# Loading rows of k four to a partition, with the column order restored in three ways

## The chip, the cores and the metric

The kernel runs on one core of one Trainium2 chip. The metric is the device time of one execution in microseconds (us), the lower the better.

## The reference

Rotary embedding on q and k, then scores of every query row against every key row, for each head. All in fp32.

```python
batch, seq, heads, dim = 16, 512, 16, 64
q_rot = concat([q1 * cos - q2 * sin, q1 * sin + q2 * cos], axis=-1)   # halves of 32
k_rot = concat([k1 * cos - k2 * sin, k1 * sin + k2 * cos], axis=-1)
scores = np.einsum('bshd,bthd->bsht', q_rot, k_rot)                   # [16, 512, 16, 512]
```

The scores are 268 MB, q and k together 67 MB: the outputs are four times the inputs.

## The kernel before

The unit of work is a *block*: 128 rows of q of one batch against all 512 rows of k, all 16 heads, 4 MB of scores. A batch has four blocks (C = 4), the run 64. q's rows lie four to a partition (row 4p + c), k's rows the other way (row 128c + p), so that k's transposed columns come out in their natural order. The price is that k can be read from HBM only in runs of 4 KB.

```python
q_v = q.rearrange("b (p c) h d -> b p c h d", c=C)
k_v = k.rearrange("b (c p) h d -> b p c h d", c=C)
o_v = out.rearrange("b (p c) h t -> b c p h t", c=C)
# ... (cut)
def load_pair(which, pair):                       # 1 MB: half a batch
    b, x = divmod(pair, C // 2)
    # ...
    src = (k_v if which == "k" else q_v)[b, :, 2 * x : 2 * x + 2]
    nc.sync.dma_start(t.rearrange("p c (h d) -> p c h d", h=H), src)
```

VectorE (DVE) rotates each piece in three passes into a separate tile, TensorE (PE) transposes it, ScalarE (ACT) or DVE copies the transposes to `kT` and `qT`. Then the scores, a head pair at a time, on two 64-row halves of PE side by side (eight of these instructions took 1.92 us in the trace):

```python
def scores(i, p, st):
    # ... (cut)
    for r in range(2):
        nc.tensor.matmul(out=ps[:, r, :], lhsT=lhs[64 * r : 64 * r + 64, :],
                         rhs=rhs[64 * r : 64 * r + 64, :], start=True, stop=True)
    nc.scalar.copy(out=st[:, 2 * p : 2 * p + 2, :], in_=ps)
    # ...
    elif b > 0 and p == HP - 1:
        nc.sync.dma_start(o_v[b, i % C], st)      # one 4 MB store per block
```

There are three staging tiles `st`. One 1 MB load is issued after each block.

## Time and profile before

| | before |
|---|---|
| time, median of 3 | 808.65 us (808.45 to 809.09) |
| share of the DMA queue's packets in 16 engines' time | 98.2% |
| PE, ACT, DVE busy | 85%, 69%, 65% |
| one block in the steady stretch | 12.46 us |
| one block when nothing but PE limits it | 10.02 us |

In the profile's lines, "L172" is the source line of an instruction, `out<-in` names what is written and read, "x8" is a count. The chain of waits goes back from the last instruction to what released each step. The prediction shows its lines and reads them. Three more, of the page (after the "|": us busy, mean ns of one, us idle before and what ended it):

```profile
DMA 61%; PE 27%; ACT 6%; DVE 2%; issue 1%; ACTq 0%
...
L179 ACT COPY st<-ps 128x1024 f32<-128x1024 f32 x512 | 494.8, 1019 | 213.5 <-DMA out_dram<-st 145.1
L172 PE MATMUL ps<-kT_t,qT_t 64*128 64x512 f32 x2048 | 546.5, 647 | 82.6 <-ACT st L179 82.6
```

### The profile page before, as it was taken

What the parts mean: (1) busy time and instruction counts of PE and PEld (TensorE: products, weight loads), DVE (VectorE), ACT (ScalarE), POOL (GpSimd) and SP (SyncE); (2) the same over time, 40 slices, a digit from 0 to 9 for tenths busy, and PEclk for the clock granted to TensorE, in tenths of its full rate; (3) what the DMA queues carried; (4) which work ended last, traced back from release to release, by engine and by line L of the source; (5) the groups of instructions that cost most, each with busy time, mean ns of one, the idle gap of its engine ahead of it and who ended that gap; (6) DMA issues with size and microseconds to landing.
All of it is one profiled execution on the core that took longest, in us unless ns stands there. A gap on an engine that the chain in (4) does not pass through costs nothing.

```text
span 809.9 us, 7719 instructions
## 1 busy us (share of the span) xinstructions
PE 689.5 (85%) x3072; PEld 295.6 (36%) x3072; DVE 522.6 (65%) x508; ACT 561.8 (69%) x649; POOL 0.7 (0%) x6
## 2 busy tenths in 40 slices
PE   4989998898888888888879799797988989889870
PEld 3444443343333333333334333343333333333320
DVE  7899786655767656756568575576755856565400
ACT  4888886676767776767767668676767666777670
POOL 0000000000000000000000000000000000000000
PEclk9999999989999999999999999998989899999895
DMA  9999999999999999999999999999999999999995
GB/s 346 424 424 441 410 420 435 431 419 439 433 420 437 430 423 436 431 424 438 430 422 436 431 424 438 425 429 437 387 431 398 426 410 430 388 367 392 412 415 222
DMA packets 26916, 336.31 MB, mean 415 GB/s; under 512 B 3328, under 2 KB 4608, under 8 KB 13312
## 3 DMA queue, kind: packets, MB, share of 16 engines
q1 hardware_dynamic: 25536, 335.55, 98.2%
q8 instruction: 24, 0.39, 0.2%
q10 hardware_dynamic: 1344, 0.26, 0.2%
q14 instruction: 12, 0.10, 0.0%
HBM read 67.37 MB, written 268.44 MB: 415 GB/s over the span
## 4 chain that ended last, share of the span: by engine, by line
DMA 61%; PE 27%; ACT 6%; DVE 2%; issue 1%; ACTq 0%
DMA out_dram<-st 61%; PE ps L172 20%; PE bank L149 7%; ACT st L179 6%; DVE part L131 1%; DMA cos_k<-in_cos_dram 1%; DVE kT_t L229 0%; DVE q_rot L134 0%; DVE k_rot L134 0%; DVE k_rot L128 0%; DVE q_rot L128 0%; ACTq L300 0%; ACTq L179 0%
## 5 line engine op out<-in xcount | busy, mean ns | idle before, releaser
L179 ACT COPY st<-ps 128x1024 f32<-128x1024 f32 x512 | 494.8, 1019 | 213.5 <-DMA out_dram<-st 145.1
L172 PE MATMUL ps<-kT_t,qT_t 64*128 64x512 f32 x2048 | 546.5, 647 | 82.6 <-ACT st L179 82.6
L172 PEld LDWEIGHTS ps<-kT_t,qT_t 64*128 64x128 f32 x2048 | 180.7, 195 | 277.8 <-ACT st L179 145.5
L128 DVE TENSOR_TENSOR q_rot<-q_sb,cos_q 128x1024 f32<-128x1024 f32 x60 | 73.3, 1221 | 163.4 <-DMA q_sb<-in_q_dram 163.4
L267 DVE COPY qT_t<-bank 128x512 f32<-128x512 f32 x118 | 80.9, 686 | 78.9 <-PE bank L149 78.7
L149 PEld LDWEIGHTS bank<-ident,q_rot 128*128 128x128 f32 x512 | 60.3, 154 | 106.8 <-issue 85.6
L149 PE MATMUL bank<-ident,q_rot 128*128 128x128 f32 x512 | 92.8, 311 | 2.6 <-DVE q_rot L134 2.6
L149 PE MATMUL bank<-ident,k_rot 128*128 128x128 f32 x512 | 83.8, 288 | 11.1 <-DVE k_rot L134 10.8
L149 PEld LDWEIGHTS bank<-ident,k_rot 128*128 128x128 f32 x512 | 54.6, 142 | 104.9 <-issue 52.2
L134 DVE TENSOR_TENSOR k_rot<-k_rot,part 128x1024 f32<-128x1024 f32 x64 | 78.3, 1224 | 2.1
L134 DVE TENSOR_TENSOR q_rot<-q_rot,part 128x1024 f32<-128x1024 f32 x64 | 77.8, 1215 | 0.2
L128 DVE TENSOR_TENSOR k_rot<-k_sb,cos_k 128x1024 f32<-128x1024 f32 x60 | 73.1, 1218 | 0.0
L131 DVE TENSOR_TENSOR part<-k_sb,ss_k 128x1024 f32<-128x1024 f32 x60 | 73.0, 1217 | 0.0
L131 DVE TENSOR_TENSOR part<-q_sb,ss_q 128x1024 f32<-128x1024 f32 x60 | 72.9, 1215 | 0.0
L269 ACT COPY kT_t<-bank 128x512 f32<-128x512 f32 x112 | 66.8, 597 | 0.0
L128 DVE TENSOR_TENSOR k_rot<-early,cos_k 128x1024 f32<-128x1024 f32 x4 | 4.9, 1220 | 5.0 <-DMA cos_k<-in_cos_dram 5.0
L189 ACT COPY qT_t<-bank 128x512 f32<-128x512 f32 x10 | 5.6, 616 | 3.0 <-PE bank L149 3.0
L189 ACT COPY kT_t<-bank 128x512 f32<-128x512 f32 x10 | 5.5, 604 | 2.0 <-PE bank L149 2.0
L229 DVE COPY kT_t<-bank 128x512 f32<-128x512 f32 x6 | 4.1, 686 | 2.6 <-PE bank L149 2.6
L128 DVE TENSOR_TENSOR q_rot<-early,cos_q 128x1024 f32<-128x1024 f32 x4 | 4.9, 1217 | 0.0
L131 DVE TENSOR_TENSOR part<-early,ss_q 128x1024 f32<-128x1024 f32 x4 | 4.9, 1216 | 0.0
L131 DVE TENSOR_TENSOR part<-early,ss_k 128x1024 f32<-128x1024 f32 x4 | 4.9, 1215 | 0.0
(11 smaller groups left out, 3.4 us busy)
## 6 DMA issues: line engine op xcount, KB each, us to landing
out_dram<-st SPq DMA_DIRECT2D x60, 4096.0 KB, 27.7
k_sb<-in_k_dram SPq DMA_DIRECT2D x30, 1024.0 KB, 30.2
q_sb<-in_q_dram SPq DMA_DIRECT2D x30, 1024.0 KB, 28.8
out_dram<-st SPq DMA_DIRECT2D x16, 1024.0 KB, 11.3
early<-in_k_dram SPq DMA_DIRECT2D x1, 1536.0 KB, 9.1
early<-in_q_dram SPq DMA_DIRECT2D x1, 1536.0 KB, 12.4
early<-in_k_dram SPq DMA_DIRECT2D x1, 512.0 KB, 4.0
early<-in_q_dram SPq DMA_DIRECT2D x1, 512.0 KB, 5.5
```

What stands on the lines that cost most here:

```text
L128: lambda: nc.vector.tensor_tensor(a.rearrange(v1, **k1), src.rearrange(sv, j=HD), cs, op=mult),
L131: lambda: nc.vector.tensor_tensor(bt.rearrange(v1, **k2), src.rearrange(sv, j=D), ss, op=mult),
L134: lambda: nc.vector.tensor_tensor(a4, a4, swapped, op=add),
L149: nc.tensor.transpose(bank[:, x, :], src, ident)
L172: nc.tensor.matmul(out=ps[:, r, :], lhsT=lhs[64 * r : 64 * r + 64, :], rhs=rhs[64 * r : 64 * r + 64, :], start=True, stop=True,)
L179: nc.scalar.copy(out=st[:, 2 * p : 2 * p + 2, :], in_=ps)
L189: nc.scalar.copy(out=dst, in_=bank)
L229: nc.vector.tensor_copy(out=dst, in_=bank)
L267: nc.vector.tensor_copy(out=dst, in_=bank)
L269: nc.scalar.copy(out=dst, in_=bank)
```

## The change

The intent: read k as q is read, four rows to a partition, so that whole batches come in single 2 MB loads with runs of 16 KB; rotate in place, which frees the tiles for the rotated copies. But then column 128c + p of the transposed k belongs to row 4p + c, and the scores' columns must be put right: by PE's read of k, by PE's write to PSUM, or by ACT's read of PSUM. The change uses each in a third of the batches.

```diff
-    k_v = k.rearrange("b (c p) h d -> b p c h d", c=C)
+        "k": k.rearrange("b (p c) h d -> b p c h d", c=C),
 ...
+        t = in_pool.tile([P, C, H * D], fp32, tag=which + "_in", name=which + "_sb")
+        batches[which, b] = t
+        nc.sync.dma_start(t.rearrange("p c (h d) -> p c h d", h=H), dram[which][b])
 ...
+        def products():
+            nc.vector.tensor_tensor(pv, xs, ss, op=mult)
+            nc.vector.tensor_tensor(xc, xc, cs, op=mult)          # in place
 ...
         for r in range(2):
+            po, rh = ps[:, r, :], rhs[64 * r : 64 * r + 64, :]
+            if b > 0 and b % 3 == 1:                              # PE reads with a hop
+                rh = rh.rearrange("e (c t) -> e t c", c=C)
+                po = po.rearrange("s (t c) -> s t c", c=C)
+            elif b > 0 and b % 3 == 2:                            # PE writes with a step
+                rh = rh.rearrange("e (c t) -> e c t", c=C)
+                po = po.rearrange("s (t c) -> s c t", c=C)
 ...
+        if b > 0 and b % 3 == 0:                                  # ACT reads with a hop
+            so = so.rearrange("s r (t c) -> s r t c", c=C)
+            si = si.rearrange("s r (c t) -> s r t c", c=C)
 ...
-            if i % 2 == 1:
-                load_pair("q", (i + 1) // 2 + 2)
-            else:
-                load_pair("k", (i + 4) // 2 + 3)
+            if i % C == C - 2:
+                load("q", i // C + 2)
+            elif i % C == C - 1:
+                load("k", i // C + 3)
```

The first batch, which is loaded by heads, restores its order in the copies of the transposes; it is left out here.

More of the change, by code (lines that the diff above doesn't have):

```diff
@@ L34 @@
     in_pool = ctx.enter_context(tc.tile_pool(name="in", bufs=2))
-    rot_pool = ctx.enter_context(tc.tile_pool(name="rot", bufs=2))
+    part_pool = ctx.enter_context(tc.tile_pool(name="part", bufs=1))
     kt_pool = ctx.enter_context(tc.tile_pool(name="kt", bufs=2))
@@ L40 @@
     ps_t_pool = ctx.enter_context(tc.psum_pool(name="ps_t", bufs=2))
-    q_v = q.rearrange("b (p c) h d -> b p c h d", c=C)
-    k_v = k.rearrange("b (c p) h d -> b p c h d", c=C)
+    dram = {
+        "q": q.rearrange("b (p c) h d -> b p c h d", c=C),
+        "k": k.rearrange("b (p c) h d -> b p c h d", c=C),
+    }
     o_v = out.rearrange("b (p c) h t -> b c p h t", c=C)
     ident = const_pool.tile([P, P], fp32, name="ident")
-    tabs = {}
-    def load_tables(which, pat):
-        for name, src in (("cos", cos), ("sin", sin)):
-            t = const_pool.tile([P, C, HD], fp32, name=f"{name}_{which}")
-            nc.scalar.dma_start(t, src.rearrange(pat, c=C))
-            tabs[name, which] = t
-    def build_table(which):
-        ss = const_pool.tile([P, C, 2, HD], fp32, name=f"ss_{which}")
-        nc.scalar.copy(out=ss[:, :, 0, :], in_=tabs["sin", which])
-        nc.scalar.mul(ss[:, :, 1, :], tabs["sin", which], -1.0)
-        tabs["ss", which] = ss.rearrange("p c x j -> p c (x j)")
-    in_tiles = {}
-    IN_BUFS = {"k": 3, "q": 2}
-    def in_tile(which, pair):
-        t = in_pool.tile(
-            [P, 2, H * D], fp32, tag=which + "_in", bufs=IN_BUFS[which], name=which + "_sb"
-        )
-        in_tiles[which, pair] = t
-        return t
+    cos_t = const_pool.tile([P, C, HD], fp32, name="cos_t")
+    sin_t = const_pool.tile([P, C, HD], fp32, name="sin_t")
+    ss_t = const_pool.tile([P, C, 2, HD], fp32, name="ss_t")
+    ss_v = ss_t.rearrange("p c x j -> p c (x j)")
     st_first = [stage_pool.tile([P, H, S], fp32, tag="stage", name="st") for _ in range(2)]
@@ L77 @@
     units = {}
+    used = [0]
     def load_units(which, head, heads):
         n = C * heads * D
-        t = early[:, load_units.used : load_units.used + n]
-        load_units.used += n
-        t = t.rearrange("p (c e) -> p c e", c=C)
-        src = (k_v if which == "k" else q_v)[0, :, :, head : head + heads, :]
+        t = early[:, used[0] : used[0] + n].rearrange("p (c e) -> p c e", c=C)
+        used[0] += n
+        src = dram[which][0, :, :, head : head + heads, :]
         nc.sync.dma_start(t.rearrange("p c (h d) -> p c h d", d=D), src)
@@ L87, in load_units, with load @@
             units[which, (head + h) // G] = t[:, :, D * h : D * (h + G)]
-    load_units.used = 0
-    def load_pair(which, pair):
-        b, x = divmod(pair, C // 2)
+    batches = {}
+    def load(which, b):
         if b >= B:
             return
-        t = in_tile(which, pair)
-        src = (k_v if which == "k" else q_v)[b, :, 2 * x : 2 * x + 2]
-        nc.sync.dma_start(t.rearrange("p c (h d) -> p c h d", h=H), src)
-    rots = {}
+        t = in_pool.tile([P, C, H * D], fp32, tag=which + "_in", name=which + "_sb")
+        batches[which, b] = t
+        nc.sync.dma_start(t.rearrange("p c (h d) -> p c h d", h=H), dram[which][b])
@@ L102, in rope @@
     def rope(which, n):
-        a = rot_pool.tile([P, H * D], fp32, tag="rot_" + which, name=which + "_rot")
-        bt = rot_pool.tile([P, H * D], fp32, tag="part", name="part")
-        cs, ss = tabs["cos", which], tabs["ss", which]
+        part = part_pool.tile([P, H * D], fp32, tag="part", name="part")
         if n < C:
-            src = units[which, n]
-            sv = "p c (g j) -> p c g j"
-            v1 = "p (c g j) -> p c g j"
-            k1 = {"c": C, "j": HD}
-            cs = cs.unsqueeze(2).to_broadcast((P, C, 2 * G, HD))
-            ss = ss.unsqueeze(2).to_broadcast((P, C, G, D))
-            k2 = {"c": C, "j": D}
-        else:
-            src = in_tiles[which, n // 2][:, n % 2]
-            sv = "p (g j) -> p g j"
-            v1 = "p (g j) -> p g j"
-            k1 = {"j": HD}
-            cs = cs[:, n % C].unsqueeze(1).to_broadcast((P, 2 * H, HD))
-            ss = ss[:, n % C].unsqueeze(1).to_broadcast((P, H, D))
-            k2 = {"j": D}
@@ L124, in rope @@
-        swapped = bass.AP(bt.tensor, bt.offset + HD, [bt.ap[0], (D, H), (-HD, 2), (1, HD)])
-        a4 = a.rearrange("p (h x j) -> p h x j", x=2, j=HD)
-        rots[which, n] = a
-        return [
-            lambda: nc.vector.tensor_tensor(
-                a.rearrange(v1, **k1), src.rearrange(sv, j=HD), cs, op=mult
-            ),
-            lambda: nc.vector.tensor_tensor(
-                bt.rearrange(v1, **k2), src.rearrange(sv, j=D), ss, op=mult
-            ),
-            lambda: nc.vector.tensor_tensor(a4, a4, swapped, op=add),
-        ]
+            x = units[which, n]
@@ new lines, in rope @@
+            sv, k1, k2 = "p c (g j) -> p c g j", {"j": HD}, {"j": D}
+            cs = cos_t.unsqueeze(2).to_broadcast((P, C, 2 * G, HD))
+            ss = ss_v.unsqueeze(2).to_broadcast((P, C, G, D))
+            pv = part.rearrange("p (c g j) -> p c g j", c=C, j=D)
+            x5 = x.rearrange("p c (h x j) -> p c h x j", x=2, j=HD)
+            p5 = part.rearrange("p (c h x j) -> p c h x j", c=C, x=2, j=HD)
+            adds = [(x5[:, :, :, y], p5[:, :, :, 1 - y]) for y in range(2)]
+        else:
+            x = batches[which, n // C][:, n % C]
+            sv, k1, k2 = "p (g j) -> p g j", {"j": HD}, {"j": D}
+            cs = cos_t[:, n % C].unsqueeze(1).to_broadcast((P, 2 * H, HD))
+            ss = ss_v[:, n % C].unsqueeze(1).to_broadcast((P, H, D))
+            pv = part.rearrange(sv, **k2)
+            x4 = x.rearrange("p (h x j) -> p h x j", x=2, j=HD)
+            swapped = bass.AP(part.tensor, part.offset + HD, [part.ap[0], (D, H), (-HD, 2), (1, HD)])
+            adds = [(x4, swapped)]
@@ L137, with sums, transposed @@
+        xs, xc = x.rearrange(sv, **k2), x.rearrange(sv, **k1)
+        def products():
+            nc.vector.tensor_tensor(pv, xs, ss, op=mult)
+            nc.vector.tensor_tensor(xc, xc, cs, op=mult)
+        def sums():
+            for y, z in adds:
+                nc.vector.tensor_tensor(y, y, z, op=add)
+        return [products, sums]
     kT = {}
     qT = {}
-    def transposed(which, n, g):
-        rot = rots[which, n]
+    def transposed(which, n, g, copy):
         bank = ps_t_pool.tile([P, 4, P], fp32, tag="ps_t", name="bank")
@@ L145, in transposed @@
             if n < C:
-                src = rot.rearrange("p (c e) -> p c e", c=C)[:, x, P * g : P * (g + 1)]
+                src = units[which, n][:, x, P * g : P * (g + 1)]
             else:
-                src = rot[:, P * (4 * g + x) : P * (4 * g + x + 1)]
+                src = batches[which, n // C][:, n % C, P * (4 * g + x) : P * (4 * g + x + 1)]
             nc.tensor.transpose(bank[:, x, :], src, ident)
+        src = bank
         if which == "q":
@@ L157, in transposed @@
                 kT[b] = kt_pool.tile([P, HP, S], fp32, tag="kT", name="kT_t")
-            t = kT[b].rearrange("p h (c t) -> p h c t", c=C)
-            dst = t[:, 2 * n + g] if n < C else t[:, 4 * g : 4 * g + 4, n % C]
-        return bank, dst
+            if n < C:
+                dst = kT[b][:, 2 * n + g].rearrange("p (t c) -> p t c", c=C)
+                src = bank.rearrange("p c t -> p t c")
+            else:
+                dst = kT[b][:, 4 * g : 4 * g + 4, P * (n % C) : P * (n % C + 1)]
+        copy(out=dst, in_=src)
     def scores(i, p, st):
@@ L171, in scores @@
         for r in range(2):
-            nc.tensor.matmul(
-                out=ps[:, r, :],
-                lhsT=lhs[64 * r : 64 * r + 64, :],
-                rhs=rhs[64 * r : 64 * r + 64, :],
-                start=True,
-                stop=True,
-            )
-        nc.scalar.copy(out=st[:, 2 * p : 2 * p + 2, :], in_=ps)
+            po, rh = ps[:, r, :], rhs[64 * r : 64 * r + 64, :]
[5 more added lines that the diff above has]
+                po = po.rearrange("s (t c) -> s c t", c=C)
+            nc.tensor.matmul(
+                out=po, lhsT=lhs[64 * r : 64 * r + 64, :], rhs=rh, start=True, stop=True
+            )
+        so, si = st[:, 2 * p : 2 * p + 2, :], ps
+        if b > 0 and b % 3 == 0:
+            so = so.rearrange("s r (t c) -> s r t c", c=C)
+            si = si.rearrange("s r (c t) -> s r t c", c=C)
+        nc.scalar.copy(out=so, in_=si)
         if b == 0 and p % 2 == 1:
@@ L187, in tr_act @@
         for g in range(2):
-            bank, dst = transposed(which, n, g)
-            nc.scalar.copy(out=dst, in_=bank)
+            transposed(which, n, g, nc.scalar.copy)
     def run(ops):
@@ L195 @@
     with tc.manual_schedule():
-        load_tables("k", "(c p) j -> p c j")
-        load_tables("q", "(p c) j -> p c j")
+        for t, src in ((cos_t, cos), (sin_t, sin)):
+            nc.scalar.dma_start(t, src.rearrange("(p c) j -> p c j", c=C))
         for head, heads in ((0, G), (G, H - G)):
@@ L200 @@
             load_units("q", head, heads)
-        load_pair("k", 2)
-        load_pair("q", 2)
-        load_pair("k", 3)
+        load("k", 1)
+        load("q", 1)
         make_identity(nc, ident)
-        build_table("k")
-        build_table("q")
-        run(rope("k", 0))
-        tr_act("k", 0)
-        run(rope("q", 0))
-        tr_act("q", 0)
+        nc.scalar.copy(out=ss_t[:, :, 0, :], in_=sin_t)
+        nc.scalar.mul(ss_t[:, :, 1, :], sin_t, -1.0)
+        for which in ("k", "q"):
+            run(rope(which, 0))
+            tr_act(which, 0)
         for i in range(C):
             st = st_first[i] if i < 2 else stage_pool.tile([P, H, S], fp32, tag="stage", name="st")
-            late = []
-            if i > 0:
-                late = [("k", C + i - 1, 0), ("k", C + i - 1, 1)]
             if i < C - 1:
@@ L225 @@
                 scores(i, p, st)
-                if p in (0, 1) and late:
-                    bank, dst = transposed(*late.pop(0))
-                    dve.pop(0)()
-                    nc.vector.tensor_copy(out=dst, in_=bank)
-                if i == 0 and p == 1:
-                    load_pair("k", 4)
-                if i == 0 and p == 3:
-                    load_pair("q", 3)
+                if p in (0, 1) and i > 0:
+                    run(dve[:1])
+                    dve = dve[1:]
+                    transposed("k", C + i - 1, p, nc.vector.tensor_copy)
+                if p == 3 and i < 2:
+                    load("kq"[i], 2)
                 if p in (2, 6):
-                    m = len(dve) - (6 if p == 2 else 3) + (-3 if i == C - 1 else 0)
+                    m = len(dve) - (4 if p == 2 else 2) - (2 if i == C - 1 else 0)
                     run(dve[:m])
@@ L239 @@
             run(dve)
-            if i == 1:
-                load_pair("k", 5)
-            elif i == 3:
-                load_pair("q", 4)
-                load_pair("k", 6)
+        load("k", 3)
         for i in range(C, NST):
@@ L262 @@
                     continue
-                bank, dst = transposed(*tr[p])
                 if tr[p][0] == "q":
@@ L266 @@
                     dve = dve[1:]
-                    nc.vector.tensor_copy(out=dst, in_=bank)
+                    transposed(*tr[p], nc.vector.tensor_copy)
                 else:
-                    nc.scalar.copy(out=dst, in_=bank)
+                    transposed(*tr[p], nc.scalar.copy)
             run(dve)
-            if i % 2 == 1:
-                load_pair("q", (i + 1) // 2 + 2)
-            else:
-                load_pair("k", (i + 4) // 2 + 3)
+            if i % C == C - 2:
+                load("q", i // C + 2)
+            elif i % C == C - 1:
+                load("k", i // C + 3)
 _INS = ['q', 'k', 'cos', 'sin']
```

## The prediction

> **What bounds the kernel now.** I read the page's head and DMA parts first, then the chain of waits, the timeline of a steady stretch and the waits. First: is any resource full?
>
> ```profile
> PE 689.5 (85%) x3072; PEld 295.6 (36%) x3072; DVE 522.6 (65%) x508; ACT 561.8 (69%) x649; POOL 0.7 (0%) x6
> ...
> DMA packets 26916, 336.31 MB, mean 415 GB/s; under 512 B 3328, under 2 KB 4608, under 8 KB 13312
> ...
> q1 hardware_dynamic: 25536, 335.55, 98.2%
> ```
>
> No compute engine is full; the DMA queue's packets fill 98.2% of the 16 engines' time. Inputs and outputs together are 335.5 MB, so the change cannot lower the bytes. Second: does the end hang on those transfers? The chain of waits in order of time (start, length, what) repeats one figure from about 120 us on:
>
> ```profile
> 158.18 28.73 DMA out_dram<-st
> ...
> 187.01 1.02 ACT st L179
> ...
> 196.08 28.20 DMA out_dram<-st
> ...
> 233.46 28.18 DMA out_dram<-st
> ```
>
> A 4 MB store takes about 28 us from issue to landing; its staging buffer is then refilled in 9.1 us (187.01 to 196.08) and stored again. There are three buffers, so one 4 MB block of scores passes each (233.46 - 196.08) / 3 = 12.46 us. With 1.05 MB of loads per block that is 5.24 MB / 12.46 us = 421 GB/s. Third: what can the compute do when no buffer is missing? The same chain earlier, before the staging buffers bind:
>
> ```profile
> 72.70 1.92 PE ps L172 x8
> ...
> 82.71 1.92 PE ps L172 x8
> ...
> 92.73 1.92 PE ps L172 x8
> ```
>
> The same place in the block recurs every 10.02 us, with PE busy throughout. So PE has 2.4 us to spare per block. Of the 10.02 us, 8 x 0.96 = 7.7 us are scores (1.92 us for 8 instructions, and four instructions are one head pair of scores) and 4 x 0.59 are transposes. ACT needs 8 copies of 1.02 us or slightly less in succession, plus two of 0.60 us: at most 9.4 us. Fourth, the waits between 160 and 484 us:
>
> ```profile
> DVE q_rot L128 <- DMA q_sb<-in_q_dram: 79.7, 13, 6.7
> ACT st L179 <- DMA out_dram<-st: 73.3, 26, 4.0
> PEld ps L172 <- ACT st L179: 68.9, 52, 3.6
> ```
>
> ACT waits 2.8 us per block for a store: that is the DMA bound seen from ACT. The longest wait, DVE for q, is the tempting one, 163 us over the run, but those rotations run a block ahead and PE loses almost nothing by it in the steady stretch.
>
> [...] the median 4 KB packet took 159 ns, 8 KB 309 ns, 32 KB 1213 ns. From 8 to 32 KB this is 904 / 24 = 37.7 ns per KB, which leaves about 8 ns fixed per packet. [...]
>
> **The change part by part.**
>
> Loads. Before, k came in 4 KB packets (30 loads of 1 MB, 256 packets each, 7,680 in all) and q in 8 KB (3,840). After, 30 loads of 2 MB carry 3,840 packets of 16 KB. A 16 KB packet should take 309 + 8 x 37.7 = 610 ns (an estimate from the two rows). Before: (7,680 x 159 + 3,840 x 309) / 16 = 76.3 + 74.2 = 150.5 us of all engines. After: 3,840 x 610 / 16 = 146.4 us. Saved: 4.1 us. Thirty fewer DMAs drop 480 completion packets of 9 ns: 0.3 us. As DMA is the bound, these 4.4 us come off the end.
>
> Prefetch. A q batch is now asked for at the end of the third block of a batch for use four blocks later, some 3 blocks or 37 us before DVE wants it, against a landing of about 30 us. So DVE's q wait should nearly vanish. It wasn't on the bound; I book 0 to 4 us for the irregular stretch from 560 to 690 us, where blocks took about 12.85 us (599.89 - 561.36 = 38.5 us per three).
>
> Rotation in place. Again three DVE passes of 1,024 elements (1.22 us each); for the first batch the sum becomes two halves of 512. Nothing on the bound: DVE stays at about 520 us. [...]
>
> Column order. k's row 4p+c now becomes column 128c+p of its transpose, and each block must put it right. In batches 1, 4, 7, 10, 13 PE reads k with a hop of 512 bytes at every element; in 2, 5, 8, 11, 14 PE writes PSUM with a step of 16 bytes; in 3, 6, 9, 12, 15 ACT reads PSUM with a hop of 512 bytes. Twenty blocks each. The sizes are the same and no instruction is added, so cost comes only from a slower element rate. Call the factor on the score matmuls f: a block takes 7.7 f + 2.36 us of PE, which reaches the DMA's 12.4 us at f = 1.30. For ACT, 8.2 f + 1.2 reaches it at f = 1.37.
>
> There is also a cushion. When a buffer comes free, two other stores and some loads still stand in the queue, 2 x 4.19 MB + 1.05 MB at 421 GB/s = 22 us, while refilling takes 9 us. So about 13 us of lateness are absorbed before the DMA idles, and each unhindered block wins back 2.4 us. At f = 1.7 in the PE-read batches alone, a block is 15.4 us, 12 us late per batch, absorbed and won back in the next eight blocks: cost near 0. At f = 2, 17.7 us: 21 us late, 8 over the cushion, times 5 batches: 40 us. At 1.7 in both PE ways, 24 us late with only four blocks (10 us) to recover: 14 x 5 = 70 us. At 1.7 in all three, ACT's block is 15.1 us, nothing is recovered, and (12 + 12 + 11) x 5 = 175 us come on.
>
> **The rivals.** (1) All three orders are free, or slow by less than 30%: 808.7 - 4.4 = 804 us, perhaps 800. [...] (2) One way is slow and the cushion hides it: 805 to 820; the page would show the slower instruction and an unchanged end. (3) The PE read at twice the time: PE becomes the bound in those batches, about 845. (4) Two or three ways slow: 870 to 980. (5) The loads, now in bursts of 2 MB, leave gaps in the queue: unlikely, as even two stores alone hold 20 us of work against 9 us of refilling.
>
> **Range and chances.** I give (1) about 0.40 and (2) 0.17, which make "within 2%" or, with luck in the irregular stretch, faster; (3) and (4) share 0.42. For more than 2% faster, 16 us would have to be found where I count 4 to 8: 0.04. The median of this lopsided mix lies a little above the free case, at 812 us; the range goes from a clean 798 to 915.
>
> **What would show it.** The page should list 16 KB loads of 2 MB, the DVE wait for q near zero, and blocks of about 12.4 us. The three kinds of score instructions settle the rest, by batch: matmuls of about 0.24 us effective in every batch and ACT copies of 1.02 us mean rival (1). Longer ones with gaps in the DMA row in the same batches mean (3) or (4). I'm wrong altogether if the blocks change length while the score instructions and the queue's packets do not, or if the packets of 16 KB take much other than 610 ns.

The sum is 808.7 - 4.4 = 804 us if all three orders are free, with 0 to 4 us less for the prefetch, and 0, 40, 70 or 175 us more if they are not. The factors 1.7 and 2 in the latter are assumed, and the chances are the author's estimate; nothing in the trace before showed how fast such an access is.

## The result and the profile after

The changed kernel took 855.22 us (median of 4, 851.76 to 855.62) against 808.59 us (808.45 to 809.09). The ratio is 1.0566, 95% interval 1.0538 to 1.0594. Here and below a ratio is the mean time of one kernel's fast runs over the mean of the other's in the same rounds, so it is not quite the ratio of the quoted medians. The times of the kernel before varied between 804.7 and 813.3 us in the later rounds.

The page after, in the parts that answer to those shown of before:

```profile
PE 794.1 (93%) x3072; PEld 292.3 (34%) x3072; DVE 544.9 (64%) x516; ACT 567.5 (67%) x647; POOL 0.7 (0%) x6
...
GB/s 355 423 415 416 275 261 359 438 425 435 424 437 310 372 414 428 432 425 435 335 346 394 431 427 439 422 438 274 372 419 433 432 425 436 316 370 419 419 430 364
...
q1 hardware_dynamic: 17376, 335.55, 93.8%
...
PE 78%; DMA 14%; DVE 3%; ACT 2%; issue 0%; ACTq 0%; DVEq 0%
```

There are 8,160 fewer packets, as planned, for the same bytes. But PE went from 689.5 to 794.1 us busy with the same 3,072 matmuls, and the end now hangs on PE (78% of the chain, DMA 14%; before 27% and 61%). The GB/s row has five holes: slices of 261 to 372 where the others, the first and the last apart, have 394 and more. Five batches read k on PE with the hop, at even distances. The chain of waits shows the block in such a batch, and then in the next one (start, length, what):

```profile
238.29 3.67 PE ps L161 x8
...
255.31 3.67 PE ps L161 x8
...
297.60 1.92 PE ps L161 x8
...
307.62 1.92 PE ps L161 x8
```

The same place in the block recurs every 17.02 us in batch 4, and every 10.02 us in batch 5, which writes PSUM with the step. Eight score instructions took 3.67 us in the one and 1.92 us in the other. For the whole cycle of batches 4, 5, 6 (from the last store of batch 3 to that of batch 6) the view by windows gives the columns: us, busy time of PE, PE's weight loads, DVE, ACT and POOL, then PE clock, DMA share, GB/s:

```profile
218.28:286.35 68.07, 68.07 (x196) 18.43 (x194) 34.80 (x33) 36.37 (x41) 0.00 (x0) 1.00 0.91 383
286.35:326.44 40.09, 40.09 (x194) 17.73 (x192) 33.59 (x32) 34.76 (x41) 0.00 (x0) 1.00 0.99 405
326.44:375.24 48.80, 43.68 (x192) 18.58 (x190) 34.26 (x33) 34.84 (x40) 0.00 (x0) 0.93 1.00 431
```

In the PE-read batch (first row) PE never rests and the DMA has gaps. In the next, PE still never rests: it is catching up. In the third the DMA is full again and PE rests for 5 us, because the staging tiles are all waiting to be stored (ACT waits 7.6 us for stores there). Each of the two limits waits for the other in turn. The cycle takes 156.96 us, though PE alone needs 4 x 17.02 + 8 x 10.02 = 148.2 us and the DMA about as much (12 x 12.37 = 148.4 us by the blocks of the all-PSUM-write kernel below).

The waits after, the longest first:

```profile
DVE qT_t L142 <- PE bank L127: 259.1, 116, 5.9
ACT st L168 <- PE ps L161: 207.7, 240, 1.7
...
ACT st L168 <- DMA out_dram<-st: 33.8, 9, 4.7
```

DVE's wait for loads of q, 163.4 us before, is gone. ACT now waits mostly for PE (207.7 us, before 51.2) and much less for stores (33.8, before 145.1).

### The profile page after: what moved, and what is told of

Its sections match the earlier page's. It is cut to its first block, busy times and chain, and to the rows that moved or that the text cites. A ratio compares the mean times of both kernels' runs of the same rounds, so it can differ in the third digit from the quotient of the medians.

```text
span 850.0 us, 7712 instructions
## 1 busy us (share of the span) xinstructions
PE 794.1 (93%) x3072; PEld 292.3 (34%) x3072; DVE 544.9 (64%) x516; ACT 567.5 (67%) x647; POOL 0.7 (0%) x6
## 2 busy tenths in 40 slices
DMA packets 17700, 336.17 MB, mean 396 GB/s; under 512 B 1792, under 2 KB 3072, under 8 KB 4096
## 4 chain that ended last, share of the span: by engine, by line
PE 78%; DMA 14%; DVE 3%; ACT 2%; issue 0%; ACTq 0%; DVEq 0%
PE ps L161 64%; PE bank L127 15%; DMA out_dram<-st 13%; ACT st L168 2%; DVE part L106 1%; DVE early L111 1%; DVE early L107 1%; DMA early<-in_k_dram 1%; DVE kT_t L142 0%; DVE k_sb L107 0%; DVE k_sb L111 0%; ACTq L276 0%; ACT kT_t L142 0%; ACTq L168 0%; DVEq L106 0%
## 5 line engine op out<-in xcount | busy, mean ns | idle before, releaser
L161 PE MATMUL ps<-kT_t,qT_t 64*128 64x512 f32 x2048 | 657.1, 764 | 21.1 <-ACT st L168 21.1
L168 ACT COPY st<-ps 128x1024 f32<-128x1024 f32 x512 | 501.3, 1019 | 250.4 <-PE ps L161 207.7
L127 PEld LDWEIGHTS bank<-ident,q_sb 128*128 128x128 f32 x480 | 52.2, 145 | 129.8 <-issue 127.9
L127 PE MATMUL bank<-ident,q_sb 128*128 128x128 f32 x480 | 81.7, 295 | 0.9 <-PE ps L161 0.9
L127 PE MATMUL bank<-ident,k_sb 128*128 128x128 f32 x480 | 78.6, 287 | 0.2 <-DVE k_sb L111 0.2
L107 DVE TENSOR_TENSOR q_sb<-q_sb,cos_t 128x1024 f32<-128x1024 f32 x60 | 73.5, 1225 | 2.1
L107 DVE TENSOR_TENSOR k_sb<-k_sb,cos_t 128x1024 f32<-128x1024 f32 x60 | 73.5, 1225 | 2.0
L111 DVE TENSOR_TENSOR k_sb<-k_sb,part 128x1024 f32<-128x1024 f32 x60 | 73.5, 1225 | 2.1
L106 DVE TENSOR_TENSOR part<-q_sb,ss_t 128x1024 f32<-128x1024 f32 x60 | 73.5, 1225 | 2.0
L106 DVE TENSOR_TENSOR part<-k_sb,ss_t 128x1024 f32<-128x1024 f32 x60 | 73.0, 1216 | 0.1
L111 DVE TENSOR_TENSOR q_sb<-q_sb,part 128x1024 f32<-128x1024 f32 x60 | 72.9, 1216 | 0.0
```

Of the source, the lines that this page charges most:

```text
L106: nc.vector.tensor_tensor(pv, xs, ss, op=mult)
L107: nc.vector.tensor_tensor(xc, xc, cs, op=mult)
L111: nc.vector.tensor_tensor(y, y, z, op=add)
L127: nc.tensor.transpose(bank[:, x, :], src, ident)
L161: nc.tensor.matmul(out=po, lhsT=lhs[64 * r : 64 * r + 64, :], rhs=rh, start=True, stop=True)
L168: nc.scalar.copy(out=so, in_=si)
```

## The experiments

The runs were made on three different chips, so each kernel is compared with runs of the kernel before on its own chip, as a ratio.

My first theory from the two profiles: only the PE read is dear (1.9 times), the two other orders are free, the loads are a small gain, and what the slow blocks cost depends on how much queued work the DMA has when they begin.

### One order for all batches: PSUM write

```diff
-            if b > 0 and b % 3 == 1:
+            if False:
-            elif b > 0 and b % 3 == 2:
+            elif b > 0:
-        if b > 0 and b % 3 == 0:
+        if False:
```

> All 60 blocks after the first batch use the PSUM-write order (step of 16 bytes on the matmul's output). Theory (only the PE read hop is dear, the loads are as estimated): blocks of about 12.4 us, matmuls at 0.96 us per head pair in every batch, no DMA gaps, 804 us (801 to 808), some 0.5% under the kernel before. Rival (the PSUM write looked free only because the DMA bound hid it in its batches): PE per block above 10.02 us where buffers are free, and a time above 812 us. Rival (the 2 MB loads in bursts cost something): 809 to 820 us with score instructions unchanged.

Measured: 801.54 us (6 runs, 801.16 to 801.93) against 807.93 us; ratio 0.9916 (0.9887 to 0.9945), correct. The groups of instructions on PE:

```profile
L161 PE MATMUL ps<-kT_t,qT_t 64*128 64x512 f32 x2048 | 546.9, 651 | 72.5 <-ACT st L168 72.4
```

The same 546 us as before the change (546.5), so a step of 16 bytes on the PSUM write costs nothing here. The chain shows 4 MB stores issued at 309.69 and 408.61 us, eight blocks apart: 12.37 us per block, DMA-bound again. So this version beats both kernels, by 0.8% (clear of noise) and by 6%. The expected 804 was 2.5 us too high.

### One order for all batches: ACT read

The same edit with the third condition as `if b > 0:` and the two others off.

> All 60 blocks use the ScalarE order (512-byte hop on its PSUM read). Theory: ACT copies stay at 1.02 us mean, 804 us (801 to 808), the same as the PSUM-write kernel within 0.3%. Rival (the hop costs ACT a little that the other batches hid): copies above 1.1 us and ACT busy above 600 us; the time moves only if a copy passes 1.37 us.

Measured: 801.50 us (6 runs), ratio 0.9915 (0.9886 to 0.9944), correct.

```profile
L168 ACT COPY st<-ps 128x1024 f32<-128x1024 f32 x512 | 495.2, 1019 | 202.6 <-DMA out_dram<-st 109.4 <-PE ps L161 78.7
```

The copies with the 512-byte hop on PSUM take the same 1,019 ns as the contiguous ones before. Both rivals fall: neither of these two orders was merely hidden by the DMA.

### One order for all batches: PE read

```diff
-            if b > 0 and b % 3 == 1:
+            if b > 0:                                   # the two other conditions: False
```

> All 60 blocks use the PE-read order. Theory (PE is the bound at 17.02 us per block in these batches, nothing else slows): 60 us to the start of the fifth block, 60 x 17.02 = 1021 us, and some 20 us for the last stores: 1095 to 1110 us, DMA busy about 72%. Rival (the read hop contends with the DMA's writes and reads of SBUF, and gets cheaper or dearer with DMA load): block length other than 17.0 us.

Measured: 1089.28 us (2 runs), ratio 1.3475. In the chain:

```profile
303.16 3.67 PE ps L161 x8
...
320.18 3.67 PE ps L161 x8
```

17.02 us per block with the DMA at 304 GB/s between 300 and 1,000 us, and 17.02 us in the changed kernel with the DMA at 383. Between these two loads of the DMA the cost of the hop does not change. The whole is 6 us below the range that I wrote down: the last store landed 11 us after its issue, where 20 were allowed, and the last four blocks, which have no k left to transpose, are shorter.

### The same three orders, block by block

```diff
-            if b > 0 and b % 3 == 1:
+            if b > 0 and i % 3 == 1:
```

and likewise for the two others.

> The same three orders in the same numbers (20 blocks each), but taken in turn block by block instead of by batch of four. Theory (a PE-read block of 17.02 us is 4.6 us late, and the queue's cushion of about 13 us absorbs it when only one comes at a time and two blocks of 10.02 us follow; mean PE block (17.02 + 2 x 10.02) / 3 = 12.35 us, just at the DMA's 12.4): 806 to 818 us. Rival (each PE-read block costs its 2.3 us share of the loss wherever it stands, for instance because its reads of SBUF disturb the DMA): 850 to 860 us as in the change.

Measured: 815.34 us (4 runs), ratio 1.0085 (1.0043 to 1.0128), correct. The same 20 slow blocks, in another order, cost 40 us less than in the change. The page says that PE is now the bound by a hair:

```profile
PE 782.1 (96%) x3072; PEld 289.1 (35%) x3072; DVE 544.9 (67%) x516; ACT 567.4 (70%) x647; POOL 0.7 (0%) x6
...
PE 93%; DVE 3%; ACT 1%; DMA 0%; issue 0%; ACTq 0%
```

PE takes (17.02 + 2 x 10.02) / 3 = 12.35 us per block, practically the DMA's own 12.37. So a slow block is mostly paid for by the DMA's backlog if fast ones follow soon. It is not free: against the kernel before, on the same chip, this version is 7 us slower and the all-PSUM-write kernel 6 us faster.

### Two slow blocks of six, three of nine

```diff
-            if b > 0 and b % 3 == 1:                    # PE reads with a hop
+            if b > 0 and i % 6 < 2:                     # of nine: i % 9 < 3
-            elif b > 0 and b % 3 == 2:                  # PE writes with a step
+            elif b > 0 and i % 6 < 4:                   # of nine: i % 9 < 6
-        if b > 0 and b % 3 == 0:                        # ACT reads with a hop
+        if b > 0 and i % 6 >= 4:                        # of nine: i % 9 >= 6
```

> The three orders in turn, two blocks each: PE reads with the hop in two blocks of six. Theory (cushion of about 13 us in the DMA queue): two such blocks are 2 x (17.02 - 12.38) = 9.3 us late, less than the cushion, so the time is that of the block-by-block kernel, 812 to 820 us. Rival (the loss grows evenly with the length of the run of slow blocks, from 815 at one to 855 at four): 828 us.

> Three blocks each: PE reads with the hop in three blocks of nine. Theory: 3 x 4.64 = 13.9 us late, at the edge of the 13 us cushion, so 815 to 824 us. Rival (even growth): 842 us.

Measured: 819.48 us (2 runs) and 817.60 us (2 runs), both correct. The loss doesn't grow evenly with the length of the run of slow blocks: it is 7 to 11 us over the kernel before for one, two and three in a row, and 47 for four (14 to 17 and 53 over the all-PSUM-write kernel, each reckoned from the kernel before on its chip). Something gives way between three and four, or in the way the change places its four.

### The hop alone, in the kernel before

```diff
+            po, rh = ps[:, r, :], rhs[64 * r : 64 * r + 64, :]
+            if b > 0 and b % 3 == 1:
+                rh = rh.rearrange("e (c t) -> e t c", c=C)
+                po = po.rearrange("s (t c) -> s t c", c=C)
```

The results are wrong: the columns were already in order.

> The kernel before, with its own loads and k order, but with the 512-byte read hop on PE in batches 1, 4, 7, 10, 13 (the columns come out in a wrong order on purpose). Theory (the whole loss is the hop, and the loads are a small gain): PE 1.84 us per head pair and 17.02 us per block in those batches, and about the time of the change plus the 6 us that its loads save: 855 to 866 us. Rival (the hop is dear only with the change's loads, for instance through the bursts of 2 MB): below 840 us.

Measured: 844.18 us (4 runs), ratio 1.0440 (1.0392 to 1.0488). The hop alone explains most of the loss, 36 of 47 us, and blocks in the slow batches are 17.02 us here too. But I had expected 855 or more, and the rival below 840; neither has it. With the loads of the kernel before, the whole takes 11 us less than with the changed loads, which are by themselves a gain of 6 us. So the hop costs 36 us with the one and 53 with the other. The store issues show where: a cycle of twelve blocks takes 152.8 to 154.4 us here, and 156.9 to 157.1 in the changed kernel.

The times at which each DMA completed, taken from the trace, say why. Without waiting for work, a 4 MB store completes 9.68 us after what stands ahead of it, and a 2 MB load 4.84. In the changed kernel's cycle from 218 us on, the third slow block's store completes 14.8 us after the one before it, although that is still ahead of any load: the queue had run dry. The two 2 MB loads are issued after the third and fourth blocks of a batch, so in a slow batch nothing but one store per 17.02 us goes into the queue until the third block. The list of DMA issues shows it (the middle row is three stores, 17.02 us apart):

```profile
219.12 0.48 SPq L79 DMA_DIRECT2D k_sb<-in_k_dram  x1
235.30 34.37 SPq L173 DMA_DIRECT2D out_dram<-st  x3
269.78 0.37 SPq L79 DMA_DIRECT2D q_sb<-in_q_dram  x1
```

Each such block takes 17.02 - 9.68 = 7.3 us from the queue's reserve, and not the 4.6 us of the theory, in which the loads are spread evenly. When the first, second and third store of this batch are issued, 12.9 and 5.6 us of work stand in the queue, and then none: it has been empty for 1.8 us. In the kernel before with the hop, each block brings 1 MB of loads as well; the reserve falls by 4.9 us a block (12.8, 7.9, 3.1 us), and the queue is empty, for 0.9 us, only at the fourth store. There the store of the third block comes 10.05 us after its predecessor, the fourth 13.1.

### The loads spread as before, in the changed kernel

```diff
             if i % C == C - 2:
-                load("q", i // C + 2)
+                load("q", i // C + 2, 0)            # half a batch, 8 KB runs
             elif i % C == C - 1:
-                load("k", i // C + 3)
+                load("k", i // C + 3, 0)
+            elif i % C == 0 and i >= 2 * C:
+                load("q", i // C + 1, 1)
+            elif i % C == 1 and i >= 2 * C:
+                load("k", i // C + 2, 1)
```

> The changed kernel, orders by batch as it has them, but from the second batch on each 2 MB load is cut in two 1 MB halves (8 KB runs) and the four halves of a batch are issued one after each block, as the kernel before does, in place of two 2 MB loads after the third and fourth block. The third and fourth blocks of every slow batch are where the DMA queue runs dry. Theory (the bursts stand on the wrong side of the slow blocks, which costs the change about 4 us in each cycle of twelve blocks: 157.0 us against 153 to 154 in the kernel before with the read hop): cycles of 153 to 154 us, and 842 to 849 us in all. Rival (placement is irrelevant, the kernel before with the hop was faster for another reason): cycles of 157 us, 853 to 859 us.

Measured: 842.50 us (4 runs), ratio 1.0434 (1.0408 to 1.0460) against 1.0566 of the change, correct; cycles of 154.8, 154.4 and 152.7 us. The windows of the same cycle:

```profile
216.30:284.50 68.20, 68.20 (x196) 18.31 (x194) 34.85 (x33) 36.22 (x42) 0.00 (x0) 1.00 0.95 402
```

PE is as full as in the changed kernel (68.20 us of 68.20), but the DMA moves 402 GB/s through the slow batch in place of 383. Smaller packets and more of them, and yet 13 us faster: the placement of the 2 MB bursts is shown to cost that much in this kernel. At its four stores of that slow batch the queue held 13.7, 8.9 and 3.9 us of work and had then been empty for 0.4 us, much as in the kernel before with the hop. In a kernel without slow blocks I see no cost of the bursts: in the all-PSUM-write run the DMA's share was 1.00 from 216 to 326 us, with the same loads at the same places.

### What the length of the runs is worth

The all-PSUM-write kernel again, and two versions of it with each 2 MB load cut in two of 1 MB, with runs of 8 KB and of 4 KB:

```diff
-        nc.sync.dma_start(t.rearrange("p c (h d) -> p c h d", h=H), dram[which][b])
+        for c in (0, 1):                            # 4 KB runs: every second row; (0, 2) with c : c + 2 for 8 KB
+            nc.sync.dma_start(t[:, c::2].rearrange("p c (h d) -> p c h d", h=H), dram[which][b][:, c::2])
```

> The all-PSUM-write kernel once more, as the partner of the two kernels with shorter runs on the same chip: 801 to 803 us.

> The all-PSUM-write kernel with every 2 MB load cut in two of 1 MB with runs of 8 KB, issued one after the other at the same place. Theory (a packet costs about 8 ns beside its bytes): 7,680 packets of 309 ns for 3,840 of 611 ns are (148.3 - 146.6) = 1.7 us more of all engines, plus 0.3 us for 30 more completions: 803 to 805 us. Rival (the size of a transfer matters by itself, or the gain came from the earlier prefetch): no change within 1 us, or more than 4 us.

> The same with two 1 MB loads of every second 4 KB run, so packets of 4 KB: 15,360 packets of 159 ns are 152.6 us against 146.6: 6.0 us plus 0.3 more, 807 to 809 us, the whole gain of the loads lost again. Rival (prefetch is what gained): 801 to 804 us.

| runs of | packets of k and q loads | time, median of 6 | ratio to before |
|---|---|---|---|
| 16 KB | 3,840 | 801.80 us | 0.9932 (0.9912 to 0.9952) |
| 8 KB | 7,680 | 803.99 us | 0.9958 (0.9940 to 0.9975) |
| 4 KB | 15,360 | 807.24 us | 0.9996 (0.9976 to 1.0015) |

Against 16 KB, the two others take 2.2 and 5.4 us more where 2.0 and 6.3 were worked out from the packets' durations (611, 309 and 159 ns in these traces). So most of the gain of the changed loads is the longer run. The packets do not account for all of it: the kernel before reads q in runs of 8 KB, so by its packets the version with 4 KB for q and k should be 2.2 us slower than it (3,840 x (2 x 159 - 309) / 16), and it is level. Some 2 us (an estimate; 1 to 4 by the interval of this ratio) may thus be the earlier prefetch, or another part of the change; no run separates them.

### Which access patterns are dear

A kernel that uses another pattern in each batch, with wrong results.

```diff
+            step = {2: 2, 3: 4, 4: 8, 5: 16}
+            pair = {6: 2, 7: 4, 8: 8}
-            if b > 0 and b % 3 == 1:
+            if b == 1 or b == 10:
...
+            elif b in step:
+                rh = rh.rearrange("e (t x) -> e x t", x=step[b])
+            elif b in pair:
+                rh = rh.rearrange("e (c t x) -> e t c x", c=C, x=pair[b])
+            elif b == 9:
+                rh = rh.rearrange("e (a t) -> e t a", a=2)
+            elif b == 11:
+                po = po.rearrange("s (c t) -> s t c", c=C)
...
+        if b == 12:
+            so = so.rearrange("s r (t c) -> s r c t", c=C)
```

The other side of each access stays contiguous.

> One access pattern for each batch, results wrong on purpose, read from the length of a back-to-back head pair of score matmuls (0.96 us plain, 1.84 with the hop). [...] If every jump costs about the same (0.88 us / 512 = 1.7 ns): runs of 2, 4, 8 cost 1.4, 1.18, 1.07. Batch 11 writes PSUM with a 512-byte hop: 0.96 if a PSUM write of fp32 is free at any step. Batch 12 lets ACT write SBUF with a 16-byte step: copies of 1.02 us if ACT is free there too, 1.7 us or more if SBUF is what hurts. Batches 10 and 13 to 15 are controls: 1.84 and 0.96.

The table has the start-to-start time of head pairs of score matmuls that run back to back (the 10th percentile of each batch's 31, as the longer ones include transposes between). Written in this measure, the 0.96 and 1.84 us of the expectation are 0.86 and 1.75. The state of this single run is unknown, but its controls agree: the changed kernel's own trace has 858 and 1,746 to 1,747 ns in the same measure.

| batch | what PE reads, or what is written | ns per head pair |
|---|---|---|
| 14, 15 | contiguous | 858 |
| 1, 10 | a 512-byte hop at every element | 1746 |
| 2 | step of 8 bytes | 919 |
| 3, 4, 5 | steps of 16, 32, 64 bytes | 1800, 1837, 1721 |
| 6 | runs of 2 elements, then a hop of 512 bytes | 903 |
| 7, 8 | runs of 4 and of 8 elements, then a hop | 859, 858 |
| 9 | two regions 1 KB apart in turn | 1080 |
| 11 | PSUM written with a 512-byte hop | 876 |

In batch 12 ACT reads PSUM contiguously and writes SBUF with a step of 16 bytes. Its group in that stretch, and the one of batch 13, contiguous, from the same view:

```profile
L179 ACT COPY st<-ps 128x1024 f32<-128x1024 f32 x30 | 57.2, 2089 | 0.0
...
L179 ACT COPY st<-ps 128x1024 f32<-128x1024 f32 x27 | 26.2, 1022 | 4.1 <-PE ps L172 3.3
```

Twice the time (2,089 against 1,022 ns). So the dear accesses here were on SBUF: PE's read (1,746 ns per head pair with the hop, 858 contiguous) and ACT's write. On PSUM the three patterns tried were free, or within about 2%: PE's writes with a step of 16 bytes (546.9 us of score matmuls against 546.5) and with a hop of 512 bytes (876 ns per head pair against 858), where the shortest pair took 858 ns as well, and ACT's reads with that hop (1,019 ns, as before).

The expectation's fixed price per jump falls: by it runs of two would have taken about 1.5 times as long (858 + 888 / 2 = 1,302 ns; the 1.4 of the expectation was a little low), and they took 903. Two adjacent elements in a run, or a step of 8 bytes (919 ns), were enough to bring nearly the full rate, while steps of 16 to 64 bytes took 2.0 to 2.1 times as long. Two far regions in turn (batch 9) came out between, at 1.26. Why the rate changes where it does, no run here shows.

## Why the prediction was right or wrong

**What bounds the kernel, and the budget of a block: right.** 10.02 us for PE and about 12.4 for the DMA stood up in every run that had the pattern for it.

**The loads: right.** 16 KB packets took 611 ns (610 estimated). The gain of 4.4 us was measured as 6 us in the runs without slow blocks, with steps by run length that follow the packets' durations. DVE's wait for q vanished and may have been worth some 2 us, inside the 0 to 4 that were booked. (DVE's busy time, put at about 520 us, was 544.9; it bounds nothing.)

**The column order: the step that failed is the weight on the free case.** The prediction gave 0.40 to all three being free, an estimate that nothing in the trace before could test. For PSUM this held, on PE's writes (546.9 us of score matmuls with the step, 546.5 without) and on ACT's reads (1,019 ns a copy with the hop, as without). For PE's read of SBUF it did not: f is (17.02 - 2.36) / 7.7 = 1.90 (back to back 1,746 / 858 = 2.03: the prediction's 0.96 us per head pair is a mean over blocks with transposes in between). The rival that came true is the third, PE read at about twice the time, which it put at 845 us; its stated 812 lay between two branches, and the range to 915 held the result only because the branches were listed.

**The cushion: right in kind, wrong in size.** One, two or three slow blocks in a row are mostly absorbed (815 to 819 us), four are not. But with f = 1.90 the prediction's own rule gives (4 x 4.64 - 13) x 5 = 28 us, so about 832. The change measured 855. Two terms make up the difference, 12 and 13 us where 23 are missing. First, the cushion was taken as always full. By the store issues, the first twelve blocks of the changed kernel took 17.8 us longer than those of the all-PSUM-write kernel, nearly the whole lateness of a slow batch (18.6): at the first store of the first slow batch the queue held 1.4 us of work, at the same place of the later ones 11.7 to 12.9. The full 13 us would have left 5.6. This is read from the traces; no run tests it by itself. Second, rival (5), bursts of loads, was called unlikely for lack of gaps. With fast blocks that was right. With a slow batch the bursts come two blocks too late, and spreading them took 855.2 us to 842.5: 13 us. With spread loads the rule comes near: it gives 12 x 12.37 + 5.6 = 154.0 us for a cycle, and 152.7 to 154.8 were measured.

**Faster by over 2%: rightly unlikely.** The best version found is 0.8% under the kernel before.

## What to carry to other kernels

Before changing a layout to make a transfer a little cheaper, ask which engine pays for putting the order right and on which memory it does so: here the same permutation was free on PSUM (546.9 us of score matmuls against 546.5, ACT's copies 1,019 ns in both) and doubled the time on SBUF (1,746 ns per head pair against 858). Here a phase slower than the bound was absorbed only as far as the queue held work at its start (7 to 11 us lost over the kernel before with one to three slow blocks in a row, 47 with the change's four), so look at the length of slow phases and at what is issued during them, not at the average. And when three ways are mixed in one kernel, run each alone: without one of them there was no loss, and either of the two others beat the kernel before.

## What the runs leave open

In the changed kernel 4 MB stores completed every 9.68 us (433 GB/s) wherever work stood ahead of them, but in runs whose queue never ran dry this rose to 9.95 to 10.0 us after a while: from 124 us on in the kernel before, from 239 (but for two stores near 290 and 300) and 458 us in two traces of the all-PSUM-write kernel. In the changed kernel and with the hop in the kernel before, whose queues ran dry in every slow batch, it stayed at 9.7 us. With three slow blocks of nine it rose to 9.8 to 10.0 us from about 250 us on and was 9.7 again after a gap at 430 us. No run here settles the cause; it is worth up to 0.3 us per block, so it also makes the DMA's time per block in this document, 12.37 to 12.46 us, uncertain by that much.
